# Down product of an FFN: from fp32r halves per column tile to fp16 halves per pair of column tiles

## The chip, the cores and the metric

The kernel runs on one core of a Trainium2 chip. The metric is the device time of one execution in microseconds (us): the median of three runs of the kernel before is 3261.4 us (3257.7 to 3261.48). TensorE multiplies (PE in the profile, its weight loads PEld), VectorE is DVE, ScalarE is ACT, GpSimd is POOL, and the sync engine SP issues the DMAs.

## The reference

One encoder block over 2064 positions (16 meta tokens and 2048 real ones, 1024 features): RMS norm, one input projection, two groups of attention heads, output projection and residual, then the feed-forward part that this change touches:

```python
h = rms_norm(x, ffn_norm_g[l])
g = jnp.einsum('bld,df->blf', h, w_gate[l])
u = jnp.einsum('bld,df->blf', h, w_up[l])
x = x + jnp.einsum('blf,fd->bld', jax.nn.silu(g) * u, w_down[l])
return x[:, N_META:]
```

The width of the feed-forward part is 2816, that is 22 column tiles of 128 (NF = 22 in the kernel). All inputs and the output are float32.

## The kernel before

To keep float32 accuracy on a faster format, the kernel writes each operand as a sum of a high and a low half (`split`: ACT casts the high half, POOL subtracts it from the source to get the low one), and replaces each product by three matmuls: high by high, high by low, low by high. Gate and up products do so in fp16, after the weights were scaled by a power of two (`wsc`); the down product does so in fp32r, which needs no scale.

The feed-forward part is the block `with ExitStack() as p4`, after the output projection (L1286). The 2048 tokens are taken in two blocks `b` of 1024 (TB = 8 token tiles of 128), and for each block a loop runs over the 22 column tiles `f`. One turn of the loop, an iteration:

- `wload` brings gate, up and down weights of tile f: a DMA on SP into a raw tile (L1328), for gate and up a scaling on ACT (L1330), then the split on ACT (L113) and POOL (L117).
- For each half `n` of the block (512 tokens), 24 matmuls make the gate tile `pg` and 24 the up tile `pu` in PSUM (L1380): 96 matmuls of 512 columns in an iteration.
- ACT takes tanh (L1382), DVE two multiplications (L1383, L1384), and the result `th` is split into the fp32r pair `ah`, `al`.
- `down` of the iteration before follows: for each of 8 token tiles and 2 halves of the output width one PSUM tile `psd` with 3 matmuls of 512 columns (L1341), 48 in an iteration, and one DVE addition into the running sum `y` (L1343), 16 in an iteration. After the last f of a block the sums go out by DMA.

PSUM is fully taken: four banks for gate and up (`psG`), three for the down product (`psD`), one for transposes (`psT`). SBUF tiles that are used in turn come from rings (`place`).

The order on each engine is not written by hand here. A scheduler places each instruction by the order of the program, and an instruction that is ready goes ahead of an earlier one that still waits for an operand or a PSUM bank. The engines then run their lists strictly in that order. So the down product of one iteration, which has a place ahead of the next iteration's gate product, takes PE whenever one of its three banks is free, and gate and up matmuls fill the time between.

Of the kernel before, what the change touches and what calls it, by code (L numbers as in the profile page):

```python
# [11 lines left out]
F32 = mybir.dt.float32  # L12
F32R = mybir.dt.float32r
F16 = mybir.dt.float16
BF16 = mybir.dt.bfloat16
I32 = mybir.dt.int32
AF = mybir.ActivationFunctionType
ALU = mybir.AluOpType
AX = mybir.AxisListType
PSUM = bass.MemoryType.PSUM  # L20

P = 128
D = 1024
# [6 lines left out]
KD = D // P  # L30
UW = 384
DFF = 2816
NF = DFF // P
# [53 lines left out]
def block_kernel(ctx: ExitStack, tc: tile.TileContext, x, meta, g1, w_in, gpack, lam4, subln,  # L87
                 w_out, g2, w_gate, w_up, w_down, rope, out):
    nc = tc.nc
    V, A, G, T, SP = nc.vector, nc.scalar, nc.gpsimd, nc.tensor, nc.sync  # L90
# [4 lines left out]
    mhalf = const.tile([P, 8], F32, name="mhalf")  # L95
# [16 lines left out]
    def copy(eng, o, i):  # L112
        (A.copy if eng is A else eng.tensor_copy)(o, i)  # L113

    def split(hi, lo, src, hi_eng, lo_eng):
        copy(hi_eng, hi, src)
        lo_eng.tensor_tensor(out=lo, in0=src, in1=hi if hi.dtype == F16 else hi.bitcast(F32), op=ALU.subtract)  # L117
# [37 lines left out]
    def slot(tag, shape, dtype):  # L155

        z = ktp.tile(shape, dtype, name=tag, tag=tag)
        slots[id(z)] = tag
        keep.append(z)
        return z  # L160
# [6 lines left out]
    with ExitStack() as ph:  # L167
# [26 lines left out]
        for tag in ["kt0", "qa0", "e0", "kt1", "qb0", "kt2", "e1", "e2", "e3", "kt3", "qa1", "qb1", "e4", "e5"]:  # L194
            n, size = (2, 2 * 4 * P) if tag[0] == "q" else (5, L)
            z = slot(tag, [P, size], F32R)
            wrow += [z[:, i * UW:(i + 1) * UW] for i in range(n)]
        while len(wrow) < 2 * NU * KD:
            z = c1.tile([P, min(KD, 2 * NU * KD - len(wrow)), UW], F32R, name=f"w{len(wrow)}")
# [4 lines left out]
        for i in range(NU):  # L204
            for k in range(KD):
                raw = rows[(i * KD + k) % len(rows)]
# [138 lines left out]
        for i, (ui, t) in enumerate(order):  # L345
            hb, tab, rs = ready[t]
            pj = proj(ui, t, hb, rs)
            if ui == (PU if t in TOK[:2] else min(3, ORA - 1) if t == TOK[-2] else 3) and t != TOK[0] and t != TOK[-1]:
                n = TOK[TOK.index(t) + 1]
# [3 lines left out]
            if len(pend) > PEND:  # L353
# [6 lines left out]
                b=[slot(f"qb{i}", [P, 2, 2, 2 * P], F16) for i in range(2)])  # L360
# [18 lines left out]
    with ExitStack() as ph:  # L379
# [4 lines left out]
        def buffers(n, make):  # L384

            return [[0.0, make(i)] for i in range(n)]
# [4 lines left out]
            p=buffers(NP16, lambda i: ac.tile([P, NB * P], F16, name=f"p16_{i}")),  # L391
# [762 lines left out]
        while True:  # L1154
# [11 lines left out]
            t, n, z = best  # L1166
# [10 lines left out]
    with ExitStack() as ph:  # L1177
        yp = ph.enter_context(tc.tile_pool(name="yp", bufs=1, side="right", reuse_waits="tile"))
        TB = NT // 2
# [6 lines left out]
        wsc = yp.tile([P, 2], F32, name="wsc")  # L1186
        unh = yp.tile([P, 2], F32, name="unh")
        allones = yp.tile([P, P], F32, name="allones")
        V.memset(allones, 1.0)
        wsq = yp.tile([P, NT, 2], F32, name="wsq")  # L1190
        g2_sb = yp.tile([P, D], F32, name="g2_sb")

        def normed(np_, yt, h):
# [19 lines left out]
        with ExitStack() as p3:  # L1213
# [56 lines left out]
            cur = (*first[0], mxt[0][1])  # L1270
            pend = []
            for t in range(NT):
# [15 lines left out]
                for n in range(2):  # L1288
                    ns = slice(n * 512, (n + 1) * 512)
# [5 lines left out]
                    ps = pss.pop(0)  # L1295
                    yt = y[t] if t < TB else xt
# [5 lines left out]
                if t + 1 < NT:  # L1302
                    cur = nh + (nxt[1],)
# [4 lines left out]
        with ExitStack() as p4:  # L1308
            er, (we, wk_) = [slots[id(z)] for z in ering], (first["w"], first["wk"])
            rings = dict(w=[er[0], we[0], er[1], wk_[0]], d=[we[1], wk_[1]], a=[we[2], wk_[2]], y=[we[3], wk_[3]],  # L1310
                         r=[slots[id(z)] for t in (NT - 2, NT - 1) for z in mxt[t]])

            def place(ring, shape, dtype):
                tag = rings[ring].pop(0)
                rings[ring].append(tag)
                return slot(tag, shape, dtype)

            tp4 = p4.enter_context(tc.tile_pool(name="tp4", bufs=2, reuse_waits="tile"))
            np4 = p4.enter_context(tc.tile_pool(name="np4", bufs=1, reuse_waits="tile"))
            psT = p4.enter_context(tc.tile_pool(name="psT4", bufs=1, space=PSUM, reuse_waits="tile"))  # L1320
            psG = p4.enter_context(tc.tile_pool(name="psG", bufs=4, space=PSUM, reuse_waits="tile"))
            psD = p4.enter_context(tc.tile_pool(name="psD", bufs=3, space=PSUM, reuse_waits="tile"))

            def wload(src, name):
                dn = name == "d"
                w = place("d" if dn else "w", [P, 2, 1, D] if dn else [P, 2, KD, P], F32R if dn else F16)
                raw = place("r", [P, 1, D] if dn else [P, KD, P], F32)
                SP.dma_start(raw[:, 0] if dn else raw, src)  # L1328
                if not dn:
                    A.activation(raw, raw, AF.Copy, scale=wsc[:, 0:1])  # L1330
                split(w[:, 0], w[:, 1], raw, A, G)
                return w[:, 0], w[:, 1]

            def down(b, f, act, wd):
                ah, al = act
                for i in range(TB):
                    for n in range(2):
                        ns = slice(n * 512, (n + 1) * 512)
                        ps = psD.tile([P, 512], F32, name="psd")
                        for ii, (a, w) in enumerate(((ah, wd[0]), (ah, wd[1]), (al, wd[0]))):  # L1340
                            T.matmul(ps, a[:, i * P:(i + 1) * P], w[:, 0, ns], start=(ii == 0), stop=(ii == 2))  # L1341
                        yt = y[i]
                        V.tensor_tensor(out=yt[:, ns], in0=ps, in1=yt[:, ns], op=ALU.add)  # L1343
                    if f == NF - 1:
                        t = b * TB + i
                        SP.dma_start(out[t * P:(t + 1) * P, :], y[i])
                        if b == 0:
                            SP.dma_start(y[i], y_scr[i * P:(i + 1) * P, :])

            yn = {}  # L1350

            def pre_norm(t):
                if t % 2 == 0:
                    yn["y"] = place("y", [P, 2, D], F32)
                yn[t] = yn["y"][:, t % 2]
                SP.dma_start(yn[t], y_scr[(t - TB) * P:(t - TB + 1) * P, :])
                normed(np4, yn[t], yn[t])

            prev, turns = None, []
            for b in range(2):  # L1360
                for f in range(NF):
                    if b == 0 and f >= NF - 1 - HT and f < NF - 1:
                        pre_norm(TB + f - (NF - 1 - HT))
                    fs = slice(f * P, (f + 1) * P)
                    wg = wload(w_gate[:, fs].rearrange("(k p) n -> p k n", p=P), "g")
                    wu = wload(w_up[:, fs].rearrange("(k p) n -> p k n", p=P), "u")
                    wd = wload(w_down[fs, :], "d")
                    ac_ = place("a", [P, 2, TB * P], F32R)
                    ah, al = ac_[:, 0], ac_[:, 1]
                    for n in range(2):  # L1370
                        ns = slice(n * 512, (n + 1) * 512)
                        pg = psG.tile([P, 512], F32, name="pg")
                        pu = psG.tile([P, 512], F32, name="pg")
                        for ps, w in ((pg, wg), (pu, wu)):
                            for k in range(KD):
                                if turns and b and k % TK == TK - 1:
                                    t, q = turns.pop(0)
                                    turned(psT, t, yn[t], q)
                                for ii, (a, b_) in enumerate(((w[0], hh[n]), (w[0], hl[n]), (w[1], hh[n]))):
                                    T.matmul(ps, a[:, k], b_[:, k], start=(k == 0 and ii == 0), stop=(k == KD - 1 and ii == 2))  # L1380
                        th = tp4.tile([P, 512], F32, name="th4")
                        A.activation(th, pg, AF.Tanh, scale=unh[:, 0:1])  # L1382
                        V.scalar_tensor_tensor(th, th, 1.0, pg, op0=ALU.add, op1=ALU.mult)  # L1383
                        V.scalar_tensor_tensor(th, th, unh[:, 1:2], pu, op0=ALU.mult, op1=ALU.mult)  # L1384
                        split(ah[:, ns], al[:, ns], th, A, G)
                        if b == 0 and f == NF - 1:
                            for t in range(TB + n * HT, TB + (n + 1) * HT):
                                if n == 0:
                                    turned(psT, t, yn[t])
                                else:  # L1390
                                    turns += [(t, q) for q in range(KD // 4)]
                            if n == 0:
                                for t in range(TB + HT, NT):
                                    pre_norm(t)
                    if prev is not None:
                        down(*prev)
                    prev = (b, f, (ah, al), wd)
            down(*prev)


# [69 lines left out]
```

## Time and profile before

| | us |
|---|---|
| median of 3 runs | 3261.4 |
| profiled execution, whole | 3266.65 |
| profiled execution, span from first to last instruction | 3264.9 |
| PE busy in the span | 3130.3 |
| DVE, ACT, POOL busy | 2085.0, 1651.0, 1574.2 |
| mean granted PE clock | 0.989 of full |

The profile is of one execution. Its busy times are sums over a span with several stages, so the stage of the change has to be read alone: the feed-forward part runs from 1839.6 us, where the first gate matmul starts, to the end. In a row of the timeline the first two columns are start and length; a matmul's length is modelled and reaches into the next one, so the pace of matmuls is read from start to start. A number in square brackets is the idle time of the engine before the instruction, and behind the arrow what ended it.

### The profile page before, as it was taken

Reading aid. Unit: us, or ns where it says so; the run is one execution under the profiler, and the core shown is the slowest. Engines: PE = TensorE matmul, PEld = TensorE weight load, DVE = VectorE, ACT = ScalarE, POOL = GpSimd, SP = SyncE. Lnnn points to the kernel's source line nnn. Section 1 sums busy time; section 2 is a strip of 40 time slices with the busy share of each in tenths; the row PEclk is TensorE's granted clock in tenths of the full one; section 3 lists DMA queues with packets and bytes.
Section 4 is the critical chain, followed back from the end, with each engine's and each line's share of the span. In section 5 each row is a group of like instructions: output and inputs, shape, how many; then the busy total and the mean of one; then the engine's idle time right before and its main releaser. Section 6 shows DMA issues by size and latency. Waiting matters only on the chain.

```text
span 3264.9 us, 57936 instructions
## 1 busy us (share of the span) xinstructions
PE 3130.3 (96%) x23043; PEld 2065.4 (63%) x23043; DVE 2085.0 (64%) x3694; ACT 1651.0 (51%) x1988; POOL 1574.2 (48%) x1562
## 2 busy tenths in 40 slices
PE   8999998989988998999899999999999999999999
PEld 7999984556655565666677655555555555555555
DVE  7555568999999999999854244444444534444445
ACT  6333327888988998999864322222222322222220
POOL 6888875866666667666511322323223223223231
PEclk9999999999999999999999999999999999999999
DMA  5322233343434344433685411112111511111111
GB/s 170 72 69 68 68 74 71 80 112 78 95 93 104 82 96 98 91 89 76 169 288 185 152 49 45 59 39 59 43 55 51 175 39 59 46 52 51 46 46 52
DMA packets 503361, 281.37 MB, mean 86 GB/s; under 512 B 330704, under 2 KB 478624, under 8 KB 502576
## 3 DMA queue, kind: packets, MB, share of 16 engines
q1 hardware_dynamic: 501376, 275.14, 31.4%
q8 instruction: 181, 2.97, 0.4%
q10 hardware_dynamic: 1712, 2.51, 0.3%
q14 instruction: 92, 0.75, 0.1%
HBM read 168.44 MB, written 39.93 MB: 64 GB/s over the span
## 4 chain that ended last, share of the span: by engine, by line
PE 80%; DVE 10%; DMA 4%; issue 3%; ACT 2%; POOL 1%; SPq 0%; DVEq 0%; ACTq 0%; POOLq 0%
PE pg L1380 27%; PE psd L1341 14%; PE pl L270 11%; PE sy L483 5%; PE ob L595 5%; PE oa L571 5%; PE sy L513 3%; PE sy L514 3%; PE ps L1286 3%; DVE e L490 3%; DVE mna L503 2%; PE sy L499 2%; DVE e L537 2%; DMA wq<-in_w_gate_dram 1%; PE pt L130 1%
## 5 line engine op out<-in xcount | busy, mean ns | idle before, releaser
L1343 DVE TENSOR_TENSOR y<-psd,y 128x512 f32<-128x512 f32 x704 | 484.7, 691 | 550.8 <-PE psd L1341 548.8
L1380 PE MATMUL pg<-h2h,e 128*128 128x512 f16 x2112 | 659.9, 380 | 1.5 <-POOL e L117 1.5
L562 POOL TENSOR_TENSOR hl<-et,hl 128x1024 f16<-128x1024 f32 (+1 forms) x217 | 447.7, 2082 | 244.5 <-ACT hl L113 154.4
L1380 PEld LDWEIGHTS <-e 128*128 128x128 f16 x3168 | 283.6, 98 | 390.0 <-issue 84.9
L1380 PE MATMUL pg<-h2l,e 128*128 128x512 f16 x1056 | 400.7, 380 | 0.0
L550 POOL TENSOR_TENSOR p<-e,p 128x516 f16<-128x516 f32 x315 | 324.1, 1062 | 106.9 <-ACT p L113 89.8
L556 ACT ACTIVATE et<-sy,lnpa,ndq 128x1024 f32<-128x1024 f32 (+1 forms) x288 | 327.0, 1149 | 53.5 <-PE sy L514 24.0
L490 DVE CUSTOM_DVE_ANT_0 e<-sy,zero,mn 128x1024 f32<-128x1024 f32 x256 | 326.2, 1279 | 25.2 <-PE sy L483 22.0
L117 POOL TENSOR_TENSOR e<-qa,e 128x1024 f16<-128x1024 f32 (+1 forms) x44 | 99.9, 2269 | 497.1 <-issue 380.9
L1382 ACT ACTIVATE th<-pg,unh 128x512 f32<-128x512 f32 x88 | 60.5, 687 | 536.5 <-PE pg L1380 520.4
L483 PE MATMUL sy<-kt,qb 128*128 128x512 f16 (+1 forms) x1280 | 283.8, 342 | 42.6 <-DVE mn L490 17.0
L1341 PE MATMUL psd<-kt,kt 128*128 128x512 f32 x1056 | 323.3, 434 | 0.0
L1341 PE MATMUL psd<-e,e 128*128 128x512 f32 x1056 | 320.5, 432 | 0.7 <-DVE y L1343 0.7
L503 DVE TENSOR_REDUCE mna<-sy 128x1 f32<-128x1024 f32 x256 | 308.0, 1218 | 11.3 <-PE sy L499 9.5
L113 ACT CAST hl<-et 128x1024 f16<-128x1024 f32 (+1 forms) x288 | 276.8, 993 | 2.2
L518 ACT ACTIVATE e<-e,bs,ndq 128x2064 f32<-128x2064 f32 x128 | 269.4, 2105 | 15.7 <-DVE bs L523 14.2
L117 POOL TENSOR_TENSOR kt<-qb,kt 128x1024 fp32r<-128x1024 f32 x22 | 52.8, 2399 | 443.9 <-issue 385.2
L571 PEld LDWEIGHTS <-hl 128*128 128x128 f16 (+1 forms) x6528 | 229.0, 98 | 52.5 <-issue 15.9
L571 PE MATMUL oa<-va,hl 128*128 128x65 f16 (+3 forms) x6528 | 246.8, 194 | 6.5 <-POOL hl L562 2.3
L595 PEld LDWEIGHTS <-pt 128*128 128x128 f16 (+2 forms) x3200 | 201.7, 98 | 69.5 <-issue 6.9
L513 PE MATMUL sy<-qa,kt 128*128 128x512 f16 (+1 forms) x544 | 208.0, 382 | 33.9 <-DVE mna L503 27.9
L1341 PEld LDWEIGHTS psd<-kt,kt 128*128 128x128 f32 x1056 | 198.9, 189 | 58.9
(230 smaller groups left out, 5800.9 us busy)
## 6 DMA issues: line engine op xcount, KB each, us to landing
wq<-in_w_gate_dram SPq DMA_DIRECT2D x16, 704.0 KB, 5.6
wq<-in_w_up_dram SPq DMA_DIRECT2D x16, 704.0 KB, 5.3
qa<-in_w_gate_dram SPq DMA_DIRECT2D x22, 512.0 KB, 3.8
qa<-in_w_down_dram SPq DMA_DIRECT2D x22, 512.0 KB, 3.6
qa<-in_w_up_dram SPq DMA_DIRECT2D x22, 512.0 KB, 3.8
qb<-in_w_up_dram SPq DMA_DIRECT2D x22, 512.0 KB, 3.8
qb<-in_w_down_dram SPq DMA_DIRECT2D x22, 512.0 KB, 3.6
qb<-in_w_gate_dram SPq DMA_DIRECT2D x22, 512.0 KB, 3.8
```

The costliest lines, as they stand in the source:

```text
L270: T.matmul(ps[:rows, c0:UW], hb[:, a, k, :rows], w_at(w, ui, k)[:, c0:], start=(k == 0 and a == 0 and w == 0), stop=(k == KD - 1 and a == 1))
L483: T.matmul(y[:, (c - c0) // 512 if g_ else j, :n], qt[:, j, a, qi * P:(qi + 1) * P], kt[:, c:c + n], start=(a == 0), stop=(a == 1))
L490: V.tensor_tensor_reduce(e[:, c0:c1], src[:, :c1 - c0], zero.broadcast_to([P, c1 - c0]), 1.0, mn[:, g_ - 1:g_] if g_ else big, ALU.add, AL ...
L503: V.tensor_reduce(g["mn"][:, h, g_:g_ + 1], y.rearrange("p b n -> p (b n)"), axis=AX.X, op=ALU.min)
L550: eng.tensor_tensor(out=p[:, at + c0:at + c1], in0=st["e"][0][:, c0:c1], in1=p[:, c0:c1], op=ALU.subtract)
L556: A.activation(of(et, k), of(y, k), AF.Exp, bias=lnpa if k else lnpa[:NM], scale=ndq[:, 0:1] if k else ndq[:NM, 0:1])
L562: eng.tensor_tensor(out=of(z[:, 1], k), in0=of(et, k), in1=of(z[:, 0], k), op=ALU.subtract)
L571: T.matmul(o[:, h, :wn], z[:rows, a, i, h * P:(h + 1) * P], vt[:rows, c, vh, :wn], start=(first and h == 0 and n == 0), stop=(last and n = ...
L595: T.matmul(o, pt[:rows, blk, :], vt[:rows, c, vh, :], start=(c == 0 and n == 0), stop=(c == NC - 1 and n == 1))
L1341: T.matmul(ps, a[:, i * P:(i + 1) * P], w[:, 0, ns], start=(ii == 0), stop=(ii == 2))
L1343: V.tensor_tensor(out=yt[:, ns], in0=ps, in1=yt[:, ns], op=ALU.add)
L1380: T.matmul(ps, a[:, k], b_[:, k], start=(k == 0 and ii == 0), stop=(k == KD - 1 and ii == 2))
```

## The change

- Down weights and activations are kept unsplit at first: `wdr` (four buffers) and `th` (six). ACT squares each of them and adds up the squares (`sq4` takes the squares, `sq` the sums).
- Two column tiles f, f+1 form a pair. `scaled`, called in the first half of the next pair's first iteration, adds the sums (DVE), sums them over the partitions by a matmul with ones (`ones16`, a `psd` tile), makes power-of-two scales for activations and weights (DVE and POOL), scales the four `th` and the two `wdr` on ACT and splits each into fp16 halves (ACT, POOL).
- `down` runs once per pair: 6 matmuls add both tiles in one `psd`, so a pair has the same 96 matmuls as before but 16 DVE additions for 32, each of which multiplies by the inverse of both scales.
- Gate and up weights of the next iteration are asked for ahead of the down product.
- After the last iteration, `scaled` and `down` of the last pair follow.

```diff
-            def down(b, f, act, wd):
-                ah, al = act
+            def down(b, f, z):
                 for i in range(TB):
                     for n in range(2):
                         ns = slice(n * 512, (n + 1) * 512)
                         ps = psD.tile([P, 512], F32, name="psd")
-                        for ii, (a, w) in enumerate(((ah, wd[0]), (ah, wd[1]), (al, wd[0]))):
-                            T.matmul(ps, a[:, i * P:(i + 1) * P], w[:, 0, ns], start=(ii == 0), stop=(ii == 2))
+                        for q in range(2):
+                            for ii, (a, w) in enumerate(((0, 0), (0, 1), (1, 0))):
+                                T.matmul(ps, z["a"][:, q, a, i * P:(i + 1) * P], z["d"][:, q, w, ns], start=(q == 0 and ii == 0), stop=(q == 1 and ii == 2))
                         yt = y[i]
-                        V.tensor_tensor(out=yt[:, ns], in0=ps, in1=yt[:, ns], op=ALU.add)
+                        V.scalar_tensor_tensor(yt[:, ns], ps, z["sc"][:, 0:1], yt[:, ns], op0=ALU.mult, op1=ALU.add)
...
+            def scaled(z):
+                sc = z["sc"] = tp4.tile([P, 8], F32, name="asc")
+                s16 = tp4.tile([P, 2], BF16, name="s16")
+                V.tensor_reduce(sc[:, 6:7], z["sq"][:, 0], axis=AX.X, op=ALU.add)
+                V.tensor_reduce(sc[:, 7:8], z["sq"][:, 1, 0:2], axis=AX.X, op=ALU.add)
+                V.tensor_copy(s16, sc[:, 6:8])
+                ps = psD.tile([P, 2], F32, name="psd")
+                T.matmul(ps, ones16, s16, start=True, stop=True)
+                V.tensor_scalar(sc[:, 0:2], ps, 1e-30, None, op0=ALU.max)
+                G.tensor_tensor(out=sc[:, 2:4], in0=sc[:, 0:2], in1=mhalf[:, :2], op=ALU.pow)
+                V.tensor_scalar(sc[:, 2:4].bitcast(I32), sc[:, 2:4].bitcast(I32), 0x7F800000, None, op0=ALU.bitwise_and)
+                V.tensor_scalar(sc[:, 2:4], sc[:, 2:4], 2.0 ** 15, None, op0=ALU.mult)
+                V.reciprocal(sc[:, 4:6], sc[:, 2:4])
+                V.tensor_scalar(sc[:, 0:1], sc[:, 4:5], sc[:, 5:6], None, op0=ALU.mult)
+                for q in range(2):
+                    for n in range(2):
+                        th, ns = z["th"][2 * q + n], slice(n * 512, (n + 1) * 512)
+                        A.activation(th, th, AF.Copy, scale=sc[:, 2:3])
+                        split(z["a"][:, q, 0, ns], z["a"][:, q, 1, ns], th, A, G)
+                    A.activation(z["wdr"][q], z["wdr"][q], AF.Copy, scale=sc[:, 3:4])
+                    split(z["d"][:, q, 0], z["d"][:, q, 1], z["wdr"][q], A, G)
...
+                    wdr = wdp.tile([P, D], F32, name="wdr")
+                    SP.dma_start(wdr, w_down[fs, :])
+                    A.activation(sq4, wdr, AF.Square, accum_out=cur["sq"][:, 1, par:par + 1])
...
-                        split(ah[:, ns], al[:, ns], th, A, G)
+                        A.activation(sq4[:, :512], th, AF.Square, accum_out=cur["sq"][:, 0, 2 * par + n:2 * par + n + 1])
+                        cur["th"].append(th)
+                        if par == 0 and n == 0 and prev is not None:
+                            scaled(prev[2])
...
-                    if prev is not None:
-                        down(*prev)
-                    prev = (b, f, (ah, al), wd)
+                    if (b, f) != (1, NF - 1):
+                        wnext = gate_up((f + 1) % NF)
+                    if par == 1:
+                        if prev is not None:
+                            down(*prev)
+                        prev = (b, f, cur)
+            scaled(prev[2])
             down(*prev)
```

## Rows read from the trace of the kernel before

**Rows 1.** Page, part 1: busy us, share of the span, instructions of each engine.
```profile
PE 3130.3 (96%) x23043; PEld 2065.4 (63%) x23043; DVE 2085.0 (64%) x3694; ACT 1651.0 (51%) x1988; POOL 1574.2 (48%) x1562
```
**Rows 2.** Stretches: us, busy of PE, PEld, DVE, ACT, POOL (instructions), PEclk, DMA share, GB/s.
```profile
2400.00:2464.00 64.00, 64.00 (x289) 35.12 (x288) 27.59 (x40) 15.71 (x18) 18.07 (x11) 1.00 0.17 50
...
3237.00:3259.00 22.00, 22.00 (x96) 17.52 (x94) 21.79 (x32) 0.62 (x1) 3.55 (x3) 1.00 0.34 138
```
**Rows 3.** PE timeline, 82 fp16 matmuls without a break: first and last row.
```profile
1865.03 0.60 PE L1380 MATMUL pg<-h2h,e 128*128 128x512 f16 x2 [1.50 <-POOL e L117]
...
1882.52 0.38 PE L1380 MATMUL pg<-h2h,kt 128*128 128x512 f16 x1
```
**Rows 4.** PE timeline, fp32r matmuls of the output projection: 60 starts lie between these.
```profile
1825.25 0.39 PE L1286 MATMUL ps<-kt,e 128*128 128x512 f32 x1
...
1839.14 0.40 PE L1286 MATMUL ps<-kt,e 128*128 128x512 f32 x1
```
**Rows 5.** What PE waited for, whole span: us in total, times, longest.
```profile
PE pg L1380 <- POOL e L117: 1.5, 1, 1.5
...
PE psd L1341 <- DVE y L1343: 0.7, 1, 0.7
```
**Rows 6.** PE timeline: the first down matmuls, and all of the last two iterations.
```profile
1882.55 2.45 PE L1341 MATMUL psd<-e,e 128*128 128x512 f32 x9
...
3236.45 11.51 PE L1341 MATMUL psd<-e,e 128*128 128x512 f32 x48
...
3247.80 11.36 PE L1341 MATMUL psd<-kt,kt 128*128 128x512 f32 x48
```
**Rows 7.** Timeline of all engines around the scale of the gate and up weights.
```profile
1755.28 0.39 PE L1286 MATMUL ps<-e,e 128*128 128x512 f32 x1
...
1755.52 0.28 PE L1247 MATMUL pss<-tot,allones 128*128 128x1 f32 x2
...
1755.65 0.47 PE L1286 MATMUL ps<-e,e 128*128 128x512 f32 x1
...
1756.56 0.15 DVE L1248 TENSOR_SCALAR tot<-pss 128x1 f32<-128x1 f32 x1
...
1756.79 0.56 POOL L1249 TENSOR_TENSOR wsc<-tot,mhalf 128x1 f32<-128x1 f32 x1 [3.86 <-DVE tot L1248]
...
1758.31 0.14 DVE L1250 TENSOR_SCALAR wsc<-wsc 128x1 int32<-128x1 int32 x1
...
1758.56 0.15 DVE L1251 TENSOR_SCALAR wsc<-wsc 128x1 f32<-128x1 f32 x1
```
**Rows 8.** PE timeline around a pause in the output projection.
```profile
1735.17 1.70 PE L130 MATMUL pt<-ident,qa 128*128 128x128 f32 x8 [2.45 <-DVE h2l L117]
1736.52 0.77 PE L1286 MATMUL ps<-kt,e 128*128 128x512 f32 x1
...
1739.23 0.40 PE L1286 MATMUL ps<-kt,e 128*128 128x512 f32 x1
1739.47 0.62 PE L1286 MATMUL ps<-e,e 128*128 128x512 f32 x2
```
**Rows 9.** Groups by line: busy us, mean ns of one, idle before and its releaser.
```profile
L1343 DVE TENSOR_TENSOR y<-psd,y 128x512 f32<-128x512 f32 x704 | 484.7, 691 | 550.8 <-PE psd L1341 548.8
...
L1384 DVE SCALAR_TENSOR_TENSOR th<-th,unh,pg 128x512 f32<-128x512 f32 x85 | 63.6, 748 | 127.1 <-PE pg L1380 127.1
...
L1382 ACT ACTIVATE th<-pg,unh 128x512 f32<-128x512 f32 x88 | 60.5, 687 | 536.5 <-PE pg L1380 520.4 <-POOL e L117 16.1
...
L1330 ACT ACTIVATE qa<-qa,wsc 128x1024 f32<-128x1024 f32 x43 | 49.5, 1151 | 142.8 <-DMA qa<-in_w_up_dram 73.8 <-DMA qa<-in_w_gate_dram 69.1
L113 ACT CAST e<-qb 128x1024 f16<-128x1024 f32 x44 | 46.0, 1046 | 20.8 <-PE pg L1380 19.1 <-PE psd L1341 1.2
...
L113 ACT CAST e<-th 128x512 fp32r<-128x512 f32 x44 | 27.0, 614 | 6.8 <-DVE th L1384 6.8
...
L117 POOL TENSOR_TENSOR e<-qa,e 128x1024 f16<-128x1024 f32 x22 | 47.0, 2134 | 78.2 <-ACT e L113 78.2
```

More of the change, by code (lines that the diff above doesn't have):

```diff
@@ L1190, in block_kernel @@
         wsq = yp.tile([P, NT, 2], F32, name="wsq")
+        ones16 = yp.tile([P, P], BF16, name="ones16")
+        V.memset(ones16, 1.0)
         g2_sb = yp.tile([P, D], F32, name="g2_sb")
@@ L1316, in place @@
                 return slot(tag, shape, dtype)
-            tp4 = p4.enter_context(tc.tile_pool(name="tp4", bufs=2, reuse_waits="tile"))
+            tp4 = p4.enter_context(tc.tile_pool(name="tp4", bufs=6, reuse_waits="tile"))
+            wdp = p4.enter_context(tc.tile_pool(name="wdp", bufs=4, reuse_waits="tile"))
+            sq4 = p4.enter_context(tc.tile_pool(name="sq4p", bufs=1, reuse_waits="tile")).tile([P, D], BF16, name="sq4")
             np4 = p4.enter_context(tc.tile_pool(name="np4", bufs=1, reuse_waits="tile"))
@@ L1324, in wload, with gate_up @@
             def wload(src, name):
[L1325 to L1330, printed above, removed]
+                w = place("w", [P, 2, KD, P], F16)
+                raw = place("r", [P, KD, P], F32)
+                SP.dma_start(raw, src)
+                A.activation(raw, raw, AF.Copy, scale=wsc[:, 0:1])
                 split(w[:, 0], w[:, 1], raw, A, G)
                 return w[:, 0], w[:, 1]
-            def down(b, f, act, wd):
-                ah, al = act
+            def gate_up(f):
+                fs = slice(f * P, (f + 1) * P)
+                return [wload(w[:, fs].rearrange("(k p) n -> p k n", p=P), n) for w, n in ((w_gate, "g"), (w_up, "u"))]
+            def down(b, f, z):
                 for i in range(TB):
@@ L1359, in block_kernel @@
             prev, turns = None, []
+            wnext = gate_up(0)
             for b in range(2):
@@ L1364, in block_kernel @@
                     fs = slice(f * P, (f + 1) * P)
[L1365 to L1369, printed above, removed]
+                    wg, wu = wnext
+                    par = f % 2
+                    if par == 0:
+                        cur = dict(a=place("a", [P, 2, 2, TB * P], F16), d=place("d", [P, 2, 2, D], F16), sq=tp4.tile([P, 2, 4], F32, name="sq"), th=[], wdr=[])
+                    wdr = wdp.tile([P, D], F32, name="wdr")
+                    SP.dma_start(wdr, w_down[fs, :])
+                    A.activation(sq4, wdr, AF.Square, accum_out=cur["sq"][:, 1, par:par + 1])
+                    cur["wdr"].append(wdr)
                     for n in range(2):
```

## The prediction

> **What bounds the kernel now.** I first read the busy times: PE is busy for 96% of the span, all others for two thirds or less [rows 1]. A share over the whole span does not say what the feed-forward part is worth, so the next view is the table of stretches. Two iterations of the loop take 64.0 us there, PE is busy for all of it at the full clock, and DVE, ACT and POOL for 27.6, 15.7 and 18.1 us [rows 2]. The waits agree: in the feed-forward part PE waited once for a weight half (1.5 us) and once for an addition (0.7 us) [rows 5]. So this part is bound by the number of matmuls times the pace of one, and work on the other engines costs nothing as long as it comes in time.
>
> The pace is read from start to start. In fp16, 81 steps take 1882.52 - 1865.03 = 17.49 us, 215.9 ns each [rows 3]. In fp32r, 60 steps take 13.89 us, 231.5 ns each [rows 4]. In the stretch of two iterations, 192 gate and up matmuls at 215.9 ns make 41.45 us; the other 22.55 us belong to 96 down matmuls, 234.9 ns each [rows 2, 3]. The last 3 ns over the pure fp32r pace I take to be the changes between the two formats.
>
> The order matters too. The first down product starts at 1882.55, when the gate and up matmuls of the second iteration are done, and nine of its matmuls (three banks) go at once [rows 6]: an earlier place in the program wins PE as soon as it has a bank. The down products of the last two iterations run as blocks of 48 from 3236.45 on [rows 6], with nothing else left for PE.
>
> **The change part by part.**
>
> *Format of the down product.* The number of matmuls stays at 96 per pair. At the fp16 pace they take 96 x 215.9 = 20.73 us for 22.55: 1.82 us less per pair, 40.0 us less for 22 pairs. All of it lies on the path, since PE is the bound. Bounds: the pure difference of the two paces, 15.6 ns x 2112 = 33 us, at one end, and 41 us (19.4 ns, if the changes of format cost a little more than I read) at the other. I take 40, the stretch itself.
>
> The Trainium skill ("TensorE: Matmul & The Clock Gate", Part 2, weight-path perf modes) has a rule that speaks against this gain: the array processes one element per cell and cycle whatever its width. By it an fp32r column costs no more than an fp16 one and the 40 us are not there; the paces of 215.9 and 231.5 ns at the same full clock speak against the rule.
>
> *Matmul with ones.* One per pair on PE, 22 in all. The nearest is the matmul with ones for the gate and up scale, in two passes: from the matmul before it to the one after it are 0.37 us, of which 0.23 are that matmul, so 0.14 us [rows 7]. The new one is bf16, one pass: 0.07 to 0.14, I take 0.1, in sum 2 us. It needs a bank of the three, so it queues behind nearly all of the down product before it. By then its sums are some 30 us old, as that down product is itself spread between gate matmuls. So I price no wait in the steady part; what a wait would cost is the second rival.
>
> *Squares, scales and later splits.* Per pair ACT gets four squares and four scalings of 512 columns (at most 0.69 each by the tanh) and two squares and two scalings of 1024 (at most 1.15) [rows 9], 10.1 us, which makes 26 of 62. POOL's six down splits are the same kind as before and no longer (2.13 us for an fp16 half of 1024). DVE loses 32 x 0.69 and gains 16 x 0.75 [rows 9] and some eight instructions of 0.15 us: 9 us less. None comes near PE. On ACT, a burst of one `scaled` (9.6 us, next paragraph) stands in front of a tanh or of the next weights; the tanh has its slack in the four gate banks, half an iteration of 10.4 us (48 x 215.9 ns). I price this at nothing; with no cover it is the fourth case below. SP has the same 22 loads per weight and block; only the place of the down load changes.
>
> *Start.* The first three iterations have no down matmuls to fill gaps, and the raw ring serves two loads per iteration for three. The 1.5 us wait may go or grow: between -1.5 and +3 us, I take 0.
>
> *End.* Here the change adds an exposed chain. After the last gate and up matmuls PE has two pair products left, 2 x 20.7 us. The first (pair 20) is ready. The second needs `scaled` of the last pair, and its matmul with ones stands behind the first product in the queue for the three banks, though its sums are ready early. So PE finishes the first product and then waits for: ones and maximum, power, mask and multiplication, from 1755.52 to 1758.71 in the one like it, 3.2 us, with some other DVE work between [rows 7], taken as 3.0; then on ACT two tiles of 0.69 + 0.61 and one of 1.15 + 1.05, that is 4.8 us [rows 9], after which the first matmul can go at 7.8 us; another 4.8 us for the second tile of the pair, and POOL's last low half 2.13 us: 14.7 us. In between PE can do 12 of the 96 matmuls (nine of the first tile, three of the second, in three banks). The other 84 take 18.1 us, so the product ends 32.8 us after the first one where it would have taken 20.7 without the wait: 12.1 us lost. After a pause of 2.45 us, PE in the output projection ran from 1735.17 to 1739.23 at about half pace (six matmuls 452 ns apart, for 231.5), which is the level of 1.2 GHz, and lost 2 us [rows 8]. I add it once: 14 us. Bounds: 0, if the matmul with ones gets its bank ahead of the first product, which then hides the chain; 17, if none of the 12 early matmuls go. I take 14, because rows 6 show the earlier place in the program winning.
>
> *Sum.* -40 + 2 + 0 + 14 = -24 us. The profiled execution took 3266.65 us, 1.75 more than its span, so it would become 3242.6. It lies 5.2 us above the median of the runs; taken from the median, 3261.4 - 24 = 3237.4, so 3237 us.
>
> **The rivals.**
>
> *The end is hidden* (0.17). The bank is granted early, the chain of 14.7 us lies beside the 20.7 us of the first product: 3261.4 - 40 + 2 = 3223. For it: the scheduler lets ready work overtake. Against it: the product ahead is always ready too and has the earlier place.
>
> *PE waits at the matmul with ones in each pair* (0.06). PE takes its list in order, and behind that matmul stand the gate matmuls, whose tanh and weights then come late as well. If it stood right behind the last up matmul of its pair, it would wait for two multiplications (0.69 and 0.75), a square (0.7), two sums and a copy (0.5) and their hand-overs, about 3.2 us, and 2 us for the clock [rows 8, 9]: 5.2 us x 22 = 114 us, slower, 3237 + 114 = 3351. The change loses from 1.1 us per pair on (24 / 22). Against it: the bank it needs comes only after the down product before, and PE waited 0.7 us for banks in the whole kernel before [rows 5].
>
> *fp16 brings nothing here* (0.04). If 234.9 ns were the cost of the down product's own pattern (banks, weight changes) and not of the format, then 3261.4 + 2 + 14 = 3277, slower. This is also what the skill's rule above gives. Against it: the output projection, another pattern, shows 231.5 ns in the same format [rows 4].
>
> *The bursts show* (0.08). If ACT and POOL give gate weights or banks back half a microsecond late per pair, 11 us come back: 3248.
>
> **How the numbers follow.** The forecast has 0.65: 3237, between 3231 and 3244 by the bounds of format, start and end. With the hidden end at 3223 (3220 if format changes and the start add their 1 and 1.5 us) and the bursts at 3248, give or take 2, that is 0.90, so the range is 3220 to 3250. Both cases above it are slower: 0.10. A measurement of this kernel tells 0.2% (6.5 us) from no change: faster 0.88, same 0.03, slower 0.09, where I move a little of the slower cases to the middle for a wait of about 1 us per pair.
>
> **What would show it.** The down line should show starts 216 ns apart in fp16, and a stretch of two iterations should fall from 64.0 to 62.3 us with PE busy throughout. The matmul with ones should stand after the 16th group of a down product and PE should not wait there, except at the end: a gap of 7 to 8 us between the last two pair products, then a thin stretch to 15 us, with a clock below 1.00. I am wrong if that gap is missing (then 3223), if PE shows 22 pauses on the ones line, or if the pace of the fp16 down matmuls is not that of the gate matmuls.

## The result

The changed kernel takes 3234.45 us, the median of four runs (3233.06 to 3236.51), for 3261.44 before: a ratio of 0.9919, 95% interval 0.9902 to 0.9936, or 27 us less. The forecast was 3237.

The page of the changed kernel, part 1, to be read against [rows 1]:

```profile
PE 3091.1 (96%) x23065; PEld 1909.2 (59%) x23065; DVE 1912.2 (59%) x3519; ACT 1841.9 (57%) x2384; POOL 1566.3 (48%) x1584
```

PE is still the bound. Its weight loads and DVE lost work, ACT took 191 us more, and PE waits for it in one place only, at the very end.

The steady part first. These are rows of the PE timeline of the changed kernel: the starts of two pair products, the last group of the first of them and the matmul with ones behind it.

```profile
1916.35 4.05 PE L1348 MATMUL psd<-e,e 128*128 128x512 f16 x18
...
1947.64 1.46 PE L1348 MATMUL psd<-e,e 128*128 128x512 f16 x6
1948.94 0.17 PE L1365 MATMUL psd<-s,ones 128*128 128x2 bf16 x1
...
1978.53 4.05 PE L1348 MATMUL psd<-kt,kt 128*128 128x512 f16 x18
```

From one pair to the next are 62.18 us. The 64.0 us of [rows 2] are not the counterpart: they are the length of the window that was chosen there, and 289 matmuls touch it. Two rows of the PE timeline before, one pair of iterations apart, give the period:

```profile
2418.30 1.74 PE L1341 MATMUL psd<-e,e 128*128 128x512 f32 x6
...
2482.38 1.74 PE L1341 MATMUL psd<-e,e 128*128 128x512 f32 x6
```

That is 64.08 us, so a pair takes 1.90 us less now. Without the 192 gate and up matmuls (41.4 us), 22.6 us were left for 96 down matmuls before, 235.8 ns each.

In the changed kernel the matmul with ones stands behind the 16th group of the product, and PE does not wait there. A window of nearly one period shows the same, with the columns of [rows 2]:

```profile
2400.00:2461.90 61.90, 61.90 (x289) 28.09 (x288) 19.71 (x32) 24.16 (x36) 17.52 (x12) 1.00 0.18 51
```

PE has no gap, ACT is at 24.2 us of 62.

What the matmul with ones costs can be read from three starts elsewhere in the PE timeline:

```profile
2445.12 1.46 PE L1348 MATMUL psd<-e,e 128*128 128x512 f16 x6
2446.42 0.17 PE L1365 MATMUL psd<-s,ones 128*128 128x2 bf16 x1
2446.45 0.38 PE L1414 MATMUL pg<-h2l,e 128*128 128x512 f16 x1
```

The next matmul starts 0.03 us after it, and the period agrees: 288 matmuls at 215.8 ns make 62.15 us, and 62.18 are measured. So the change of format is worth 64.08 - 62.15 = 1.93 us per pair.

Now the waits of PE in the feed-forward part (us in total, times, longest), against [rows 5]:

```profile
PE psd L1348 <- ACT kt L113: 8.7, 1, 8.7
PE psd L1348 <- POOL e L117: 2.5, 2, 1.8
PE psd L1348 <- POOL kt L117: 2.1, 2, 1.6
PE psd L1348 <- DVE y L1350: 0.6, 1, 0.6
PE pt L130 <- DVE h2l L117: 0.6, 1, 0.6
```

The wait of gate for a weight half, 1.5 us before, is gone. The waits on ACT and on POOL's `kt` stand at the end, the other three (3.7 us) between 2512 and 2521, where the token blocks change. The end in the PE timeline, against [rows 6]:

```profile
3171.58 20.88 PE L1348 MATMUL psd<-e,e 128*128 128x512 f16 x96
3192.30 0.17 PE L1365 MATMUL psd<-s,ones 128*128 128x2 bf16 x1
3201.19 1.44 PE L1348 MATMUL psd<-kt,kt 128*128 128x512 f16 x3 [8.73 <-ACT kt L113]
3204.20 3.75 PE L1348 MATMUL psd<-kt,kt 128*128 128x512 f16 x9 [1.58 <-POOL kt L117]
3208.50 18.43 PE L1348 MATMUL psd<-kt,kt 128*128 128x512 f16 x84 [0.55 <-POOL kt L117]
```

The product of the pair before runs dense, then comes the matmul with ones, a pause of 8.7 us, a thin stretch of 3 and 9 matmuls, and the other 84 in a block that starts 16.2 us after the ones. The last product lasts from 3192.3 to 3226.8, 34.5 us where 20.7 would do: 13.7 us lost, worked out with the unrounded starts. The same end by stretches (columns of [rows 2]):

```profile
3192.30:3201.20 8.90, 0.17 (x3) 0.11 (x2) 1.54 (x6) 6.67 (x10) 2.09 (x3) 0.78 0.00 0
3201.20:3208.50 7.30, 5.18 (x12) 1.63 (x12) 0.00 (x0) 1.93 (x3) 7.25 (x5) 0.56 0.00 1
3208.50:3226.80 18.30, 18.30 (x84) 8.08 (x83) 11.08 (x15) 0.00 (x0) 0.00 (x0) 1.00 0.47 192
```

The granted clock is 0.78 over the pause and 0.56, near the level of 1.2 GHz, over the twelve thin matmuls, and it is at full over the 84.

**Where the time went.** The feed-forward part took 1425.3 us in the profile before (1839.6 to 3264.9) and 1397.8 after (1833.4 to 3231.2): 27.5 us less, near the 27.0 of the medians. The parts: format, 21 pairs at 1.93 us and the last at some 1.6, -42.1; ones, 22 x 0.03, +0.7; start, -1.5; change of blocks, idle time of 3.7 us for 0.8, +2.9; the end, +13.7; from the last matmul to the end of the program, 4.3 for 5.7, -1.4. That is -27.7 for the 27.5 measured, so no time of any size is left without a place. The spans differ by 6.2 us more, which lies ahead of the feed-forward part. Its start is no property of the change: it was 1833.4 in this profile and 1839.7 in another of the very same kernel (below). So lengths of the feed-forward part are compared from profiles, and times of kernels from medians.

### The profile page after: what moved, and what is told of

Read it like the earlier page. It is cut to its first block, busy times and chain, and to the rows that moved or that the text cites. A ratio compares the mean times of both kernels' runs of the same rounds, so it can differ in the third digit from the quotient of the medians.

```text
span 3231.2 us, 58114 instructions
## 1 busy us (share of the span) xinstructions
PE 3091.1 (96%) x23065; PEld 1909.2 (59%) x23065; DVE 1912.2 (59%) x3519; ACT 1841.9 (57%) x2384; POOL 1566.3 (48%) x1584
## 5 line engine op out<-in xcount | busy, mean ns | idle before, releaser
L1414 PE MATMUL pg<-h2h,e 128*128 128x512 f16 x2112 | 638.3, 379 | 0.0
L1414 PEld LDWEIGHTS <-e 128*128 128x128 f16 x3168 | 308.2, 98 | 370.6 <-ACT e L113 0.3
L1350 DVE SCALAR_TENSOR_TENSOR y<-psd,asc,y 128x512 f32<-128x512 f32 x352 | 261.5, 749 | 349.0 <-PE psd L1348 311.4
L1367 POOL TENSOR_TENSOR asc<-asc,mhalf 128x2 f32<-128x2 f32 x22 | 15.3, 697 | 603.1 <-DVE asc L1366 603.1
L1348 PE MATMUL psd<-kt,kt 128*128 128x512 f16 x1056 | 240.8, 381 | 10.9 <-ACT kt L113 8.7
L1348 PE MATMUL psd<-e,e 128*128 128x512 f16 x1056 | 238.2, 379 | 3.1 <-POOL e L117 2.5
L595 PE MATMUL ob<-vb,pt 128*128 128x128 f16 (+2 forms) x3200 | 233.9, 220 | 0.8 <-DMA pt<-p 0.8
L1417 DVE SCALAR_TENSOR_TENSOR th<-th,pg 128x512 f32<-128x512 f32 x88 | 60.6, 688 | 293.8 <-ACT th L1416 293.8
L1419 ACT ACTIVATE sq<-th 128x512 bf16<-128x512 f32 x88 | 55.2, 628 | 311.8 <-DVE th L1418 306.2
```

Source lines behind the costliest of these rows:

```text
L595: T.matmul(o, pt[:rows, blk, :], vt[:rows, c, vh, :], start=(c == 0 and n == 0), stop=(c == NC - 1 and n == 1))
L1348: T.matmul(ps, z["a"][:, q, a, i * P:(i + 1) * P], z["d"][:, q, w, ns], start=(q == 0 and ii == 0), stop=(q == 1 and ii == 2))
```

## The experiments

Two theories had to be told apart at each end of the sum: is the gain that of the format or of the pairing, and is the loss at the end a queue for a PSUM bank or the chain itself?

### Format alone

```diff
-                w = place("d" if dn else "w", [P, 2, 1, D] if dn else [P, 2, KD, P], F32R if dn else F16)
+                w = place("d" if dn else "w", [P, 2, 1, D] if dn else [P, 2, KD, P], F16)
...
-                    ac_ = place("a", [P, 2, TB * P], F32R)
+                    ac_ = place("a", [P, 2, TB * P], F16)
```

> The kernel before, with the down halves written as fp16 for fp32r and nothing else: one column tile at a time, no scale, no squares, no matmul with ones; what the scales do for the range of fp16 is left out. Theory (the gain is the format): 2112 matmuls at 215.9 for 234.9 ns, 40 us less and no chain at the end: 3221 us. Rival (the pace of 234.9 ns is that of the pattern, three matmuls to a bank and an addition): 3258 to 3261 us.

Measured: 3219.06 us, ratio 0.9871 (0.9857 to 0.9884), 42 us less. Its last two iterations in the PE timeline, the same 48 and 48 matmuls as in [rows 6]:

```profile
3194.28 10.52 PE L1341 MATMUL psd<-e,e 128*128 128x512 f16 x48
3204.64 10.52 PE L1341 MATMUL psd<-kt,kt 128*128 128x512 f16 x48
```

48 steps take 10.36 us, 215.8 ns each, with three matmuls to a bank as before. The gain is the format's.

### Pairing alone

```diff
-                        for ii, (a, w) in enumerate(((ah, wd[0]), (ah, wd[1]), (al, wd[0]))):
-                            T.matmul(ps, a[:, i * P:(i + 1) * P], w[:, 0, ns], start=(ii == 0), stop=(ii == 2))
+                        for q, ((ah, al), wd) in enumerate(pair):
+                            for ii, (a, w) in enumerate(((ah, wd[0]), (ah, wd[1]), (al, wd[0]))):
+                                T.matmul(ps, a[:, i * P:(i + 1) * P], w[:, 0, ns], start=(q == 0 and ii == 0), stop=(q == 1 and ii == 2))
```

(with `down` called after every second column tile, and buffers for two pairs)

> The kernel before, with the down product run once per pair of column tiles, six matmuls into one PSUM tile, but on fp32r halves as before and without scales, squares or the matmul with ones. Theory (the gain is the format): 96 down matmuls of a pair take 22.2 us (231.5 ns each, the pure pace) to 22.55 us (234.9, as before), the time is 3253 to 3262 us. Rival (the gain is the pairing: half as many PSUM tiles and additions): the down matmuls fall to 216 ns, 40 us less, 3221 us. If the 3 ns over the pure pace are changes of format, runs of 18 for 3 to 6 should take most of them away: then it is near 3255.

Measured: 3259.73 us, ratio 0.9996 (0.9987 to 1.0005): no difference that can be told. In its PE timeline, a run of 18 down matmuls shows the pace:

```profile
2642.54 0.85 PE L1342 MATMUL psd<-dx,kt 128*128 128x512 f32 x3
2643.23 0.86 PE L1342 MATMUL psd<-dx,e 128*128 128x512 f32 x3
2643.93 0.86 PE L1342 MATMUL psd<-dx,kt 128*128 128x512 f32 x3
2644.62 0.86 PE L1342 MATMUL psd<-dx,e 128*128 128x512 f32 x3
2645.32 0.86 PE L1342 MATMUL psd<-dx,kt 128*128 128x512 f32 x3
```

Twelve steps in 2.78 us are 231.7 ns each, the pure pace of the output projection [rows 4]: inside a run of fp32r matmuls the pairing makes no difference. From pair to pair this kernel takes 63.83 and 63.93 us in turn, which is 233.7 ns for a down matmul, the changes of format included, for 235.8 in the kernel before. So of the 4.3 ns above the pure pace about half went with the fewer changes between the formats, 0.2 us per pair. Neither that nor half as many additions on DVE bought anything that can be told in the time.

### The matmul with ones in another bank

```diff
-                ps = psD.tile([P, 2], F32, name="psd")
+                ps = psT.tile([P, 2], F32, name="pt")
```

> The changed kernel, with the PSUM tile of the matmul with ones taken from the bank of the transposes, which is free at the end, and not from the three banks of the down product. Theory (the pause at the end is a queue for a bank): the matmul with ones of the last pair runs within some 3 us of the last gate and up matmul, in the middle of the product of the pair before; the chain of scale, casts and low halves, 16.2 us from the ones to the last low half in the changed kernel, lies beside the 20.7 us of that product; the pause of 8.7 us and the thin stretch after it go, 13.7 us less: 3234.5 - 13.7 = 3221 us. Rival (the chain of the last pair is late by itself, its squares and sums or ACT): the pause stays and the time stays at 3234.

Measured: 3229.63 us, ratio 0.99 (0.9885 to 0.9915), 5 us less than the changed kernel, not 13.7. The intervals of the two ratios overlap, so the lengths of the feed-forward part have to decide (below). The PE timeline shows the end nearly as expected (the ones come 5.2 us after the last gate and up matmul, not 3):

```profile
3186.52 5.34 PE L1348 MATMUL psd<-e,e 128*128 128x512 f16 x24
3191.70 0.17 PE L1365 MATMUL pt<-s,ones 128*128 128x2 bf16 x1
3191.72 15.70 PE L1348 MATMUL psd<-e,e 128*128 128x512 f16 x72
3207.26 20.88 PE L1348 MATMUL psd<-kt,kt 128*128 128x512 f16 x96
```

No pause: the ones run inside the product before, and the last product is dense. But the feed-forward part took 1392.2 us (1840.2 to 3232.4), 5.6 us less than the changed kernel and 8 us more than the 1384.1 that the end alone would give. They stand at the change of blocks, where the transposes of the new block now come one after the other: PE waits 7.7 us there for 3.7, and in its stretches the granted clock falls to half, which is some 4 us more:

```profile
2521.86 1.12 PE L130 MATMUL pt<-ident,e 128*128 128x128 f32 x4 [1.40 <-DVE h2l L117]
2524.38 1.12 PE L130 MATMUL pt<-ident,kt 128*128 128x128 f32 x4 [1.40 <-DVE h2l L117]
```
```profile
2520.00:2525.00 5.00, 2.20 (x11) 1.56 (x11) 1.38 (x2) 1.17 (x2) 0.00 (x0) 0.65 0.00 0
2525.00:2530.00 5.00, 2.20 (x10) 1.40 (x9) 1.38 (x2) 1.17 (x2) 0.00 (x0) 0.50 0.00 0
```

In the changed kernel the down product of the block's last pair fills this time. Here its matmul with ones stands behind the transposes in the queue for their one bank, so that product comes too late to fill anything:

```profile
2543.49 0.17 PE L1365 MATMUL pt<-s,ones 128*128 128x2 bf16 x1
```

The queue was moved, not removed.

### All scales early

```diff
-                        if par == 0 and n == 0 and prev is not None:
-                            scaled(prev[2])
...
                     if par == 1:
+                        scaled(cur)
                         if prev is not None:
                             down(*prev)
                         prev = (b, f, cur)
-            scaled(prev[2])
             down(*prev)
```

> The changed kernel, with the scale of a pair asked for right after its second iteration, ahead of the down product of the pair before, in all 22 pairs. Theory (an instruction that is not ready is overtaken when the list is made, so PE never stands at the matmul with ones): the first bank that comes free after the sums goes to the matmul with ones, PE shows no pauses at it, and the last chain lies beside the product before it: 3221 us, as with the other bank. Rival (PE waits at the matmul with ones in each pair when it comes early): 22 pauses of about 3 us and up to 2 us each for the clock, 3221 + 66 to 114 = 3287 to 3335 us.

Measured: 3238.67 us, ratio 0.993 (0.9917 to 0.9942), some 4 us more than the changed kernel; the feed-forward part took 1401.0 us for 1397.8. Both theories missed. PE did not wait 22 times at the ones, only twice, 1.5 us at 2485 and 2.05 us at the end. In the other 20 pairs 29 gate matmuls of the next iteration stood ahead of the ones, and PE did not wait. The last product has no pause before it. But the change of blocks has the bare transposes again (8.9 us of waits for them, 7.0 of these between 2521 and 2532, and a clock of 0.50 in 2530 to 2535). The low halves of the block's last pair are done at 2504.96, well before, and yet its down product starts only here:

```profile
2572.84 0.17 PE L1365 MATMUL psd<-s,ones 128*128 128x2 bf16 x1
2572.86 2.32 PE L1348 MATMUL psd<-e,e 128*128 128x512 f16 x10
```

It starts right behind the matmul with ones of the next pair, which this order of the program puts ahead of it, and which had to wait for sums that were not yet there. So the three banks are handed out in the order of the program: a ready product does not overtake an unready matmul that asked for a bank before it. The account of the scheduler ahead of the prediction, that a ready instruction goes ahead of an earlier one that waits, has this exception.

### The last scale early

```diff
                     if par == 1:
+                        if (b, f) == (1, NF - 1):
+                            scaled(cur)
                         if prev is not None:
                             down(*prev)
                         prev = (b, f, cur)
-            scaled(prev[2])
             down(*prev)
```

> The changed kernel, with the scale of the last pair alone asked for ahead of the product of the pair before; all other pairs as in the changed kernel. Theory: the pause at the end is a queue for a bank, and what the two earlier runs (other bank; all scales early) gave back stands at the change of the token blocks, where their down product could no longer fill PE's time beside the transposes. Here that place is left as in the changed kernel, so the end gives its 13.7 us and nothing is given back: the feed-forward part takes 1397.8 - 13.7 = 1384 us, the kernel 3221 us. Rival (asking for a scale early costs PE time by itself, wherever it is): 3228 to 3238 us, as the two earlier runs showed, and the change of blocks shows no pause.

Measured: 3226.29 us, ratio 0.9891 (0.9877 to 0.9904); the feed-forward part took 1387.9 us (1836.5 to 3224.4). The end gave 10.0 us of the 13.7, and the change of blocks is as in the changed kernel. The rest is in two rows of the PE timeline, and in the stretch behind the first of them (columns of [rows 2]):

```profile
3176.75 0.16 PE L1365 MATMUL psd<-s,ones 128*128 128x2 bf16 x1 [2.05 <-DVE s L1363]
3176.77 22.57 PE L1348 MATMUL psd<-e,e 128*128 128x512 f16 x96
```
```profile
3176.77:3182.00 5.23, 5.23 (x18) 2.08 (x18) 2.29 (x7) 3.67 (x6) 0.70 (x1) 0.67 0.00 0
```

PE stands 2.05 us at the ones, with 96 ready matmuls behind it on its list, and these take 22.57 us for 20.88, since the granted clock is 0.67 over the first 5.2 us: 3.7 us together. This is the rival "PE waits at the matmul with ones", once.

The changed kernel run beside it:

> The changed kernel once more, unaltered, on the same chip as the run with the last scale early, so that the two are compared there: 3234 us, the feed-forward part 1398 us, with the pause of 8 to 9 us before the last product and some 4 us of pauses at the change of blocks.

Measured: 3234.52 us, ratio 0.9915 (0.9902 to 0.9929), the feed-forward part 1398.1 us (1839.7 to 3237.8), with the waits listed above to within 0.3 us.

### The last scale in the middle of the product before

```diff
                         V.scalar_tensor_tensor(yt[:, ns], ps, z["sc"][:, 0:1], yt[:, ns], op0=ALU.mult, op1=ALU.add)
+                    if after is not None and i == 1:
+                        scaled(after)
...
-                            down(*prev)
+                            down(*prev, after=cur if (b, f) == (1, NF - 1) else None)
                         prev = (b, f, cur)
-            scaled(prev[2])
             down(*prev)
```

> As the run with the last scale early, but asked for after the first two token tiles (four PSUM tiles) of the product of the pair before, so that the matmul with ones stands behind 24 matmuls that need no wait. Theory: of the 13.7 us at the end, the early scale gave 10.1; the other 3.7 are PE standing 2.05 us at the matmul with ones, whose sums were not there yet, and 1.7 us at the lower clock after it (96 matmuls in 22.57 us for 20.88). With work ahead of it neither happens: 1384 us for the feed-forward part, 3221 us, no wait on the ones line, both last products 20.9 us. Rival (the 3.7 us are the cost of the chain running beside a product, ports or banks): the product before the last still takes 22.5 us and the time stays at 3226.

Measured: 3219.63 us, ratio 0.9877 (0.9863 to 0.9892), 15 us less than the changed kernel. The feed-forward part took 1383.9 us (1832.7 to 3216.6), the 1384 expected. The end in the PE timeline:

```profile
3170.72 5.34 PE L1348 MATMUL psd<-e,e 128*128 128x512 f16 x24
3175.90 0.17 PE L1367 MATMUL psd<-s,ones 128*128 128x2 bf16 x1
3175.93 15.70 PE L1348 MATMUL psd<-e,e 128*128 128x512 f16 x72
3191.47 20.88 PE L1348 MATMUL psd<-kt,kt 128*128 128x512 f16 x96
```

No wait, and 24 + 72 matmuls in 20.75 us. A cost of the chain beside the product (its rival) does not exist here. This version keeps the scales and beats both kernels; format alone is as fast, without the protection of fp16's range.

### Both last scales in the middle

The same with `after=cur if f == NF - 1 else None`, and no second call of `scaled` in the next block.

> As the run before, and the same for the last pair of the first block of tokens. Theory: the waits for low halves beside the transposes at the change of blocks, 2.5 us plus 1.2 us behind them, come from the same queue for a bank, and go too: 3 to 4 us less, 3217 us. Rival (the transposes with their one bank set the pace there, whatever fills the gaps): no change against the run before, 3221 us, or more, if the down product then no longer fills the time beside the transposes, as when all scales came early (8 us of pauses and a lower clock): 3229 us.

Measured: 3221.54 us, ratio 0.9882 (0.9865 to 0.9898); the feed-forward part took 1383.2 us (1835.3 to 3218.5). No change against the run before that can be told, so the rival holds: POOL's low halves no longer keep PE, but the transposes do:

```profile
2538.58 0.66 PE L130 MATMUL pt<-ident,kt 128*128 128x128 f32 x4 [1.40 <-DVE h2l L117]
```

PE's waits there fell from 3.7 to 2.6 us; the filling work ran out before the transposes did.

## Why the prediction was right

*The sum.* The forecast of -24 us came out as -27, with the main gain and the main loss nearly as priced. Five parts were off by 1 to 3 us each, in both directions, and that they partly balance is luck: format -2.1, ones -1.3, start -1.5, the last stretch of the program -1.4, the change of blocks +2.9.

*Format: the mechanism right, the size 0.1 us per pair too small.* The forecast had 1.82 us per pair, 40 us in all, and it measured 1.93, 42 us, which is also what format alone brought. The 64.0 us that it read as two iterations were the length of the window; the period was 64.08, and a down matmul cost 235.8 ns, not 234.9. The upper bound of 41 us was passed. The pairing added nothing, and the pace of 215.8 ns came with the format alone. The Trainium skill's rule ("TensorE: Matmul & The Clock Gate", Part 2, weight-path perf modes), that the array takes one element per cell and cycle whatever its width, does not hold in this case if it is read as a price per matmul in fp32r against fp16: only the format differs between the kernel before and format alone, and a matmul takes 231.5 to 235.8 ns in the one and 215.8 in the other.

*Matmul with ones: the mechanism right, the size off.* Priced at 0.1 us, it takes 0.03 (0.7 us in sum for 2). The two passes in [rows 7] were a poor model of one pass of bf16.

*Squares and bursts on ACT: right.* PE never waited for them in the steady part, with ACT at 24.2 us of 62 (26 forecast).

*Start:* -1.5 us, at the end of its bounds.

*Change of blocks: not priced.* The forecast looked at the steady part, the start and the end. The place where the blocks change has the same chain, with transposes instead of an empty PE, and lost 2.9 us. The runs with the other bank and with all scales early show that up to 8 us more hang on it.

*End: right in sum, 13.7 for 14, by luck: two errors cancel.* The chain from ones to the last low half took 16.2 us, not 14.7. The forecast let ACT go tile by tile, with only POOL's last low half behind it; the ACT timeline of the changed kernel shows all six scalings first:

```profile
3194.53 1.33 ACT L1375 ACTIVATE th<-th,asc 128x512 f32<-128x512 f32 x2 [21.19 <-DVE asc L1369]
...
3198.03 1.13 ACT L1377 ACTIVATE wdr<-wdr,asc 128x1024 f32<-128x1024 f32 x1
3199.07 1.12 ACT L113 CAST kt<-th 128x512 f16<-128x512 f32 x2
3200.10 1.04 ACT L113 CAST kt<-wdr 128x1024 f16<-128x1024 f32 x1
```

so the first matmul went at 8.9 us, not 7.8. POOL, which starts behind the first cast, then makes its six low halves one after the other:

```profile
3199.80 2.27 POOL L117 TENSOR_TENSOR kt<-th,kt 128x512 f16<-128x512 f32 x2 [5.72 <-issue]
3202.03 2.12 POOL L117 TENSOR_TENSOR kt<-wdr,kt 128x1024 f16<-128x1024 f32 x1
3204.11 2.26 POOL L117 TENSOR_TENSOR kt<-th,kt 128x512 f16<-128x512 f32 x2
3206.33 2.12 POOL L117 TENSOR_TENSOR kt<-wdr,kt 128x1024 f16<-128x1024 f32 x1
```

They take 8.65 us, and POOL is done 5.3 us behind the last cast (2.1 in the forecast): POOL sets the end of the chain, not ACT. Against that, the clock was priced at 2 us and cost nearly nothing: the slow matmuls fell into the stretch in which PE waited for POOL anyway, and the 84 ran at 217 ns. The term should have asked whether the slow matmuls are on the path.

*The reason for the end: right.* The scale of the last pair queued for a bank behind a product. With the ones inside that product (the last scale in the middle), the end gave its 13.7 us back: 1383.9 us for the feed-forward part, for 1397.8.

*The slower rival: the price too high, the place rare.* One wait at the ones costs 2.05 + 1.7 = 3.7 us (3.2 + 2 = 5.2 forecast). It happens when the ones get a bank with no ready work ahead of them: once in the run with the last scale early, twice with all scales early, never in the changed kernel. In the steady part of the changed kernel the product of the pair before stands in front, and with all scales early the 29 gate matmuls do.

Still open: what in an fp32r matmul costs the 15.7 ns. Its weight load takes longer (a mean of 189 ns on PEld in the kernel before, 98 in fp16), but still less than a matmul, and no run separated the two operands.

## What to carry to other kernels

Where PE is busy throughout, price a change of format by the start-to-start pace of the two formats in the same trace, and count the matmuls. Read the period of a loop from two starts of the same instruction, not from the length of a window. A new small step in a chain is cheap while a large ready block stands ahead of it in each queue it uses, and it is dear at the ends of the pipeline and where stages change: go through those places one by one. When a PSUM ring is shared, ask for its banks in the order in which the operands will be ready, with some ready work ahead of a step that is not.

## What was not expected of the hardware

- At the same granted clock of 1.00, a 512-column matmul takes 231.5 ns in fp32r and 215.8 in fp16, and a down product that changes format every three to six matmuls pays some 4 ns per matmul more (235.8), one that changes after 18 about 2 (233.7).
- A matmul with 2 columns between two of 512 moves the next one by 0.03 us, though its own row says 0.17.
- A pause of 2.05 us was followed by 96 matmuls in 22.57 us for 20.88, with a granted clock of 0.67 over the first 5.2 us; after the pause of 8.7 us the granted clock was 0.56 over twelve matmuls and 1.00 over the next 84.
